# The first norm's conditioning chunks split between TensorE and VectorE, a T5 bias table built on GpSimd's queue, and a later forget bias

## The chip, the cores and the metric

One core of a Trainium2 chip runs the whole program. The metric is the device time of one execution in microseconds (us); the times below are medians of three runs. TensorE (PE) does matmuls, VectorE (DVE) elementwise work and reductions, ScalarE (ACT) activations and copies, GpSimd (POOL) small elementwise work, and SyncE (SP) issues the DMAs.

## What is computed

Two layers of a transformer block on 256 tokens of width 1024, in float32. Each layer has a mixer (three kinds of attention side by side) and a SwiGLU. A conditioning vector `c` gives, by a matmul with `w_ada`, a shift, a scale and a gate for both halves of each layer:

```python
mod = (silu(c) @ w_ada[l] + b_ada[l])
shift_a, scale_a, gate_a, shift_f, scale_f, gate_f = split(mod, 6)
h = rmsnorm(x, g_mix_pre[l]) * (1.0 + scale_a) + shift_a
x = x + gate_a * rmsnorm(mixer(h), g_mix_post[l])
h = rmsnorm(x, g_ffn_pre[l]) * (1.0 + scale_f) + shift_f
x = x + gate_f * rmsnorm(swiglu(h), g_ffn_post[l])
```

In the mixer, "fox" attention (4 heads) adds a cumulated forget logit to its scores, "moba" attention (4 heads; at 256 tokens there is one block) adds a T5 bias that depends on the distance of query and key only, and "mla" attention (8 heads) goes through low-rank latents and rope.

## The kernel before

Weights stream from HBM in pieces of 128x1024 (512 KB). `split` (lines 101 to 103) turns each into a high part `wh` on ScalarE (L102) and a low part `wl` on VectorE (L103), and a product is three matmuls (L148 to L150 or L170 to L172). The program is written as a dataflow; a planner puts each engine's instructions into one fixed order before the run, by its own estimate of when each is ready, with the order of writing as priority. An engine works through its list in that order and waits at each instruction for what it needs. SP is the only DMA issuer.

The conditioning comes in chunks. Twelve chunks per half layer: eight of 256 columns (128 of shift, 128 of scale, for one of eight groups of model columns) and four of the gate. One chunk is two loads `adaw` of 512 KB (`ada_load`, L250). There are two ways to compute one (`ada_chunk`, L260): on VectorE as two multiply-and-reduce instructions against `crow`, the conditioning vector spread over all partitions (L266), or on TensorE as eight matmuls on four column groups (L274, `adap`, two records each), a copy on ScalarE (L277, `adasb`), two transposes (L286, `adac`) and a small reduce on VectorE (L287). `on_dve` (L37) picks the way; the first norm's eight chunks of layer 0 all go by TensorE. `ada_scale` then adds the bias (L294) and forms the factor (L296) in `ab`.

Layer 0's first norm and first projection are interleaved (`phase_a`, L578, here "phase A"): for each of eight groups `kc` of model columns, the chunk is conditioned, x is transposed and normalised by a matmul with a diagonal (L949, `xT`), `modulate` (L364) makes `hv` on ScalarE and the parts `h0aH` and `h0aL` on VectorE (L367 to L369), and seven column slots are projected with three matmuls each. TensorE's order in this stage is written out by hand (`chain`): the conditioning and the transpose of group kc+1 stand before slot 0 of group kc, `adac` of kc+1 before slot 2. The diagonal needs the row factor `rs`, a power on GpSimd (L343), one for each 128 tokens.

After phase A come the latents, the values (`value1`), and the T5 bias (`t5_bias`, L226): one matmul of a one-hot table gives the band of biases by distance, four DMAs write it to DRAM 32 times per head (`scr`, L242), and one DMA (L245) reads it back with a step of 383 elements per partition, so that row p comes out shifted by p: `mobab`. The forget logits are cumulated, and `rows_of` (L299) writes them to DRAM (L306) and reads them back spread over all partitions (`gk`, L309), also on SP. `fox_bias` (L725) makes the bias of one fox head in two pieces: L729 for the first 128 queries, which is ordered after the last maximum seen so far (`last["max"]`, set at L435), and L732 for the others, which has no such order.

Then eight pairs of heads: four mla, two fox, two moba. A pair's scores (L458, L460) need `qx` (L763, VectorE) for mla; softmax is L433 to L445 on VectorE, ScalarE and GpSimd. Between the pairs stand pieces of projection (`qkp`) and the remaining conditioning chunks (`fill`).

Of the kernel before, what the change touches and what calls it, by code (L numbers as in the profile page):

```python
# [36 lines left out]
def on_dve(l, which, j):  # L37

    if which == 1 and j < KC:
        return j in MIX_DVE[l]  # L40
    return j >= KC or l > 0


@with_exitstack
def block_kernel(ctx, tc, A, out):
# [16 lines left out]
    def pm(name, n=512):  # L62
        return psum.tile([P, n], F32, tag="pm", bufs=2, name=name)
# [120 lines left out]
    x = const.tile([P, 2, D], F32, name="x")  # L184
    for t in range(2):
        SP.dma_start(x[:, t, :], A["x"][:, t, :])
    shp = const.tile([P, 896], F32, name="shp")
    tri, ones, ktab = (shp[:, i * P:(i + 1) * P] for i in range(3))
    mask, qtab = (shp[:, 384 + i * S:384 + (i + 1) * S] for i in range(2))
    bfor = const.tile([P, L, 4], F32, name="bfor")  # L190
# [32 lines left out]

    mobab = const.tile([P, 4, S], F32, name="mobab")

    def t5_bias():  # L226
        tab = wk.tile([P, 4], F32, tag="tab", bufs=1, name="tab")
        SP.dma_start(tab, A["t5"])
        oneh = wk.tile([P, 384], F32, tag="e", bufs=4, name="oneh")
        SP.dma_start(oneh, A["k_onehot"])  # L230
        trep = wk.tile([P, 4, 32], F32, tag="kt", bufs=2, name="trep")
        DVE.tensor_copy(trep, tab[:, :, None].to_broadcast([P, 4, 32]))
        tp = pg("tp")
        for hd in range(4):
            PE.matmul(tp[32 * hd:32 * hd + 32, :384], trep[:, hd, :], oneh, start=True, stop=True,
                      tile_position=(0, 32 * hd))
        band = wk.tile([P, 384], F32, tag="e", bufs=4, name="band")
        ACT.activation(band, tp[:, :384], AF.Copy)

        scr = dram.tile([4, 4, 32, 384], F32, name="scr")  # L240
        for q in range(4):
            SP.dma_start(scr[:, q, :, :], band)  # L242
        base = scr[:, :, :, :]
        toep = bass.AP(base.tensor, base.offset + 127, [[383, P], [P * 384, 4], [1, S]])
        SP.dma_start(mobab, toep)  # L245


    loaded = {}
# [11 lines left out]
    def ada_chunk(l, which, j):  # L260
        raws = loaded.pop((l, which, j), None) or ada_load(l, which, j)
        if on_dve(l, which, j):

            sb = wk.tile([P, 2], F32, tag="adasum", bufs=4, name="adasum")
            for u in range(2):
                i = DVE.tensor_tensor_reduce(out=raws[u], in0=raws[u], in1=crow, op0=ALU.mult, op1=ALU.add,  # L266
                                             scale=1.0, scalar=0.0, accum_out=sb[:, u:u + 1])
                if last.get("ffn"):
                    order_after(i, last["wl"])
            return sb  # L270
        ps = pm("adap", 256)
        for kc in range(KC):
            g = kc % 4
            chain(PE.matmul(ps[32 * g:32 * g + 32, :], crep[:, kc, :], raws[kc // 4][:, g * 256:(g + 1) * 256],  # L274
                            start=kc < 4, stop=kc >= 4, tile_position=(0, 32 * g)))
        sb = wk.tile([P, 256], F32, tag="adasb", bufs=1, name="adasb")
        ACT.activation(sb, ps, AF.Copy)  # L277
        return sb

    def ada_columns(l, which, j, sb, dst):  # L280

        if on_dve(l, which, j):
            return sb
        ps = pm("adac", 256)
        for u in range(2):
            chain(PE.transpose(ps[:, u * P:(u + 1) * P], sb[:, u * P:(u + 1) * P], ident))  # L286
        DVE.tensor_reduce(dst, ps.rearrange("p (u g r) -> p u g r", u=2, g=4)[:, :, :, 0], op=ALU.add,  # L287
                          axis=mybir.AxisListType.X)
        return dst
# [37 lines left out]
    def gate_step(l, which, j):  # L327
        ada_gate(l, which, j)

    def scale_step(l, which, kc, sb=None):  # L330
        if kc == 0:
            ABs[l, which] = act.tile([P, KC, 2], F32, tag="ab", bufs=3, name=f"ab{l}{which}")
        ada_scale(l, which, ABs[l, which], kc, ada_chunk(l, which, kc) if sb is None else sb)


# [186 lines left out]
    def mixer(l, h, prepare, fill, after):  # L522
# [55 lines left out]
        def phase_a():  # L578
# [11 lines left out]
            for kc in range(AHEAD):  # L590
                load(kc)
            state["chain"] = True
            adas[0] = ada_chunk(0, 0, 0)
            turn(0)
            scaled(0)
# [95 lines left out]
        if l == 0:  # L691
            for i, ps in enumerate(rest):
                qk_out(ps, i)
            w1.extend(value_weights(l))
            for t in range(2):
                value1(t)
            t5_bias()


        kx = act.tile([P, 8, S], F32, tag="kx", name="kx")  # L700
# [24 lines left out]
        def fox_bias(hd):  # L725
            fb = wk.tile([P, 384], F32, tag="fb", bufs=2, name="fb")
            gk = gks[:, hd]

            i = DVE.scalar_tensor_tensor(fb[:, 0:P], gk[:, 0:P], gqs[:, 2 * hd:2 * hd + 1], mask[:, P:S],  # L729
                                         op0=ALU.subtract, op1=ALU.add)  # L730
            order_after(i, last["max"])
            DVE.scalar_tensor_tensor(fb[:, P:384], gk, gqs[:, 2 * hd + 1:2 * hd + 2], mask,  # L732
                                     op0=ALU.subtract, op1=ALU.add)
            return fb

        if l == 0:
# [259 lines left out]
def _constants():  # L996
    import numpy as np
    f = np.float32
    p = np.arange(P)
    j = np.arange(S)  # L1000
    out = {}
    out["k_tri"] = (p[:, None] <= p[None, :]).astype(f)
    out["k_ones"] = np.ones((P, P), f)
    out["k_mask"] = np.where(j[None, :] <= P + p[:, None], 0.0, NEG).astype(f)
# [11 lines left out]
    oneh = np.zeros((P, 384), f)  # L1016
    oneh[np.where(dist >= 0, _bucket(dist), 32), np.arange(384)] = 1.0
    out["k_onehot"] = oneh
    shapes = np.concatenate([out.pop(k) for k in ("k_tri", "k_ones", "k_ktab", "k_mask", "k_qtab")], axis=1)
    out["shapes"] = shapes  # L1020
    return out


def _layout(inputs):
# [4 lines left out]
    o["t5"] = np.concatenate([g["t5_table"], np.full((1, 4), NEG, np.float32), np.zeros((P - 33, 4), np.float32)])  # L1029
    o["b_forget"] = g["b_forget"]  # L1030

    def kchunks(w):
# [5 lines left out]
    for l in range(L):  # L1038
        for which in range(2):
            parts = [g["w_ada"][l][:, (3 * which + i) * D:(3 * which + i + 1) * D] for i in range(3)]  # L1040
            for j in range(12):
# [5 lines left out]
                if on_dve(l, which, j):  # L1047
# [69 lines left out]
```

## Time and profile before

| | us |
|---|---|
| median of three runs | 676.29 |
| lowest and highest of them | 673.01 and 677.72 |
| the profiled execution | 677.55 |
| its span, first to last instruction | 675.7 |

The rows further down come from that one profiled execution. Times count from the span's start. A row of the timeline has start, duration, engine, line, operation, what it writes and reads, and in brackets how long the engine stood idle before it and what ended that. The chain of waits is followed back from the last instruction, each step to what released it.

### The profile page before, as it was taken

The page shows a single profiled execution, that of the slowest core. Times are in us where ns is not written, and L with a number is a line of the kernel's source. Part 1 is how long each engine was busy: PE and PEld are TensorE (multiplying, and loading weights), DVE is VectorE, ACT ScalarE, POOL GpSimd, SP SyncE. Part 2 cuts the span into 40 slices and gives each one's busy share as a digit, 9 for nine tenths or more (in the row PEclk, how much of TensorE's full clock was granted, in tenths as well). Part 3 has the DMA queues.
Part 4 walks back from the last instruction along what each step waited for, and adds up shares of the span by engine and source line. Part 5 has one row for each costly group of instructions (what it writes and reads, how often), then busy time and mean ns, then how long its engine had stood idle before and what let it go on. Part 6 is the DMA issues. An engine that isn't in the chain of part 4 may idle for free.

```text
span 675.7 us, 12112 instructions
## 1 busy us (share of the span) xinstructions
PE 638.3 (94%) x4543; PEld 564.7 (84%) x4543; DVE 451.2 (67%) x969; ACT 365.7 (54%) x758; POOL 52.8 (8%) x90
## 2 busy tenths in 40 slices
PE   7988769999999999999998999899899999999996
PEld 5877658567999999999978988768799999999994
DVE  2557277878867777797658864875878755555543
ACT  4348436868644444443467764886764444444431
POOL 1000011431000000000001011250100000000000
PEclk8999979999999999999999999999999999999999
DMA  8968586786478898898845865651568676565511
GB/s 311 407 214 287 161 315 221 266 289 214 123 255 308 288 357 307 312 325 287 303 157 173 270 229 185 219 189 64 187 196 271 223 237 182 183 185 183 185 60 63
DMA packets 44410, 155.29 MB, mean 230 GB/s; under 512 B 5136, under 2 KB 6464, under 8 KB 44352
## 3 DMA queue, kind: packets, MB, share of 16 engines
q1 hardware_dynamic: 44352, 154.52, 67.7%
q8 instruction: 36, 0.59, 0.4%
q14 instruction: 22, 0.18, 0.1%
HBM read 152.64 MB, written 1.86 MB: 229 GB/s over the span
## 4 chain that ended last, share of the span: by engine, by line
PE 76%; DVE 8%; DMA 6%; ACT 3%; POOL 3%; issue 2%; SPq 0%; DVEq 0%; POOLq 0%; ACTq 0%
PE gu L148 11%; PE gu L149 11%; PE gu L150 11%; PE y L172 8%; PE y L170 8%; PE y L171 8%; DMA adaw<-in_w_ada_dram 4%; DVE wl L103 3%; PE adap L274 2%; PE o L478 2%; DMA scr<-band 2%; POOL rs L343 1%; PE qkp L150 1%; PE s L460 1%; PE qkp L148 1%
## 5 line engine op out<-in xcount | busy, mean ns | idle before, releaser
L103 DVE TENSOR_TENSOR wl<-raw_gu,wh 128x1024 fp32r<-128x1024 f32 (+1 forms) x100 | 108.5, 1095 | 67.8 <-ACT wh L102 66.8
L102 ACT ACTIVATE wh<-raw_gu 128x1024 fp32r<-128x1024 f32 (+1 forms) x100 | 94.2, 956 | 92.0 <-PE gu L149 62.5
L148 PE MATMUL gu<-h0fL,wh 128*128 128x256 f32 x304 | 86.2, 283 | 0.0
L148 PE MATMUL gu<-h1fL,wh 128*128 128x256 f32 x304 | 86.2, 283 | 0.0
L149 PE MATMUL gu<-h0fH,wh 128*128 128x256 f32 x304 | 86.0, 283 | 0.0
L149 PE MATMUL gu<-h1fH,wh 128*128 128x256 f32 x304 | 86.0, 283 | 0.0
L150 PE MATMUL gu<-h0fH,wl 128*128 128x256 f32 x304 | 86.0, 283 | 0.0
L150 PE MATMUL gu<-h1fH,wl 128*128 128x256 f32 x304 | 86.0, 283 | 0.0
L266 DVE CUSTOM_DVE_ANT_0 adaw<-adaw,crow 128x1024 f32<-128x1024 f32 x64 | 77.9, 1227 | 11.8 <-DMA adaw<-in_w_ada_dram 11.7
L102 ACT ACTIVATE wh<-raw_dn 128x1024 fp32r<-128x1024 f32 x44 | 46.6, 1060 | 54.8 <-issue 33.3
L171 PE MATMUL y<-wh,hid 128*128 128x512 f32 x176 | 69.6, 396 | 0.0
L170 PE MATMUL y<-wh,hid 128*128 128x512 f32 x176 | 69.5, 396 | 0.0
L172 PE MATMUL y<-wl,hid 128*128 128x512 f32 x176 | 69.5, 395 | 0.0
L103 DVE TENSOR_TENSOR wl<-raw_dn,wh 128x1024 fp32r<-128x1024 f32 x44 | 53.6, 1223 | 21.8 <-ACT wh L102 21.7
L149 PEld LDWEIGHTS gu<-h1fH,wh 128*128 128x128 f32 x304 | 58.3, 192 | 0.4
L149 PEld LDWEIGHTS gu<-h0fH,wh 128*128 128x128 f32 x304 | 58.3, 192 | 0.4
L148 PEld LDWEIGHTS gu<-h1fL,wh 128*128 128x128 f32 x304 | 58.2, 192 | 0.4
L148 PEld LDWEIGHTS gu<-h0fL,wh 128*128 128x128 f32 x304 | 58.2, 192 | 0.4
L150 PEld LDWEIGHTS gu<-h1fH,wl 128*128 128x128 f32 x304 | 58.3, 192 | 0.0
L150 PEld LDWEIGHTS gu<-h0fH,wl 128*128 128x128 f32 x304 | 58.3, 192 | 0.0
L343 POOL TENSOR_TENSOR rs<-rs,mhalf 128x1 f32<-128x1 f32 x16 | 11.0, 688 | 439.4 <-DVE rs L342 439.4
L172 PEld LDWEIGHTS y<-wl,hid 128*128 128x128 f32 x176 | 33.0, 188 | 8.0
(331 smaller groups left out, 1482.2 us busy)
## 6 DMA issues: line engine op xcount, KB each, us to landing
adaw<-in_w_ada_dram SPq DMA_DIRECT2D x96, 512.0 KB
raw_gu<-in_w_gu_dram SPq DMA_DIRECT2D x88, 512.0 KB
raw_dn<-in_w_dn_dram SPq DMA_DIRECT2D x44, 512.0 KB
raw_out<-in_w_out_dram SPq DMA_DIRECT2D x16, 512.0 KB
raw_b<-in_w_b_dram SPq DMA_DIRECT2D x12, 512.0 KB
raw_a<-in_w_a_dram SPq DMA_DIRECT2D x8, 448.0 KB
raw_uq<-in_w_uq_dram SPq DMA_DIRECT2D x4, 512.0 KB
raw_vm<-in_w_vm_dram SPq DMA_DIRECT2D x4, 512.0 KB
```

The lines of the kernel that those rows point to most:

```text
L102: ACT.activation(dst_h, src, AF.Copy)
L103: return DVE.tensor_tensor(dst_l, src, dst_h.bitcast(F32), op=ALU.subtract)
L148: chain(PE.matmul(ps, w[0], x[1], start=start, stop=False))
L149: chain(PE.matmul(ps, w[0], x[0], start=False, stop=False))
L150: chain(PE.matmul(ps, w[1], x[0], start=False, stop=stop))
L170: PE.matmul(ps, x[1], w[0], start=start, stop=False)
L171: PE.matmul(ps, x[0], w[0], start=False, stop=False)
L172: PE.matmul(ps, x[0], w[1], start=False, stop=stop)
L266: i = DVE.tensor_tensor_reduce(out=raws[u], in0=raws[u], in1=crow, op0=ALU.mult, op1=ALU.add, scale=1.0, scalar=0.0, accum_out=sb[:, u:u + 1])
L274: chain(PE.matmul(ps[32 * g:32 * g + 32, :], crep[:, kc, :], raws[kc // 4][:, g * 256:(g + 1) * 256], start=kc < 4, stop=kc >= 4, tile_pos ...
L343: POOL.tensor_tensor(r, r, mhalf, op=ALU.pow)
L478: PE.matmul(o[64 * u:64 * u + 64, lo:lo + P], v[:, u * 64:(u + 1) * 64], ps[u][:, i * P:(i + 1) * P], start=start, stop=stop, tile_positio ...
```

## The change

Three parts. First, for layer 0's first norm the chunk is laid out so that its first load holds the shift's columns and its second the scale's: the shift goes by TensorE with 128 columns (8 matmuls, one transpose), the scale by one multiply-and-reduce on VectorE that writes straight into `ab`. Second, the T5 band is made at the start of the program: all its transfers are issued by GpSimd, `scr` holds the band once (4 rows of 384), two loads of 256 KB read it back with a step of one element per partition, that is, with the rows in reverse order, and later, at the old place of `t5_bias`, two matmuls with a reversed identity (`flip`, loaded with the other constants) turn it and two copies fill `mobab`. Third, both pieces of the forget bias are ordered after `last["max"]`.

```diff
+def halves(l, which, j):
+    return l == 0 and which == 0 and j < KC
...
-    def t5_bias():
-        tab = wk.tile([P, 4], F32, tag="tab", bufs=1, name="tab")
-        SP.dma_start(tab, A["t5"])
-        oneh = wk.tile([P, 384], F32, tag="e", bufs=4, name="oneh")
-        SP.dma_start(oneh, A["k_onehot"])
-        trep = wk.tile([P, 4, 32], F32, tag="kt", bufs=2, name="trep")
-        DVE.tensor_copy(trep, tab[:, :, None].to_broadcast([P, 4, 32]))
+    def t5_load():
+        tab = wk.tile([64, 4], F32, tag="tab", bufs=1, name="tab")
+        POOL.dma_start(tab, A["t5"])
+        oneh = wk.tile([64, 384], F32, tag="e", bufs=4, name="oneh")
+        POOL.dma_start(oneh, A["k_onehot"])
         tp = pg("tp")
-        for hd in range(4):
-            PE.matmul(tp[32 * hd:32 * hd + 32, :384], trep[:, hd, :], oneh, start=True, stop=True,
-                      tile_position=(0, 32 * hd))
...
-        scr = dram.tile([4, 4, 32, 384], F32, name="scr")
-        for q in range(4):
-            SP.dma_start(scr[:, q, :, :], band)
-        base = scr[:, :, :, :]
-        toep = bass.AP(base.tensor, base.offset + 127, [[383, P], [P * 384, 4], [1, S]])
-        SP.dma_start(mobab, toep)
+        PE.matmul(tp[0:4, :384], tab, oneh, start=True, stop=True)
+        band = wk.tile([4, 384], F32, tag="e", bufs=4, name="band")
+        ACT.activation(band, tp[0:4, :384], AF.Copy)
+        scr = dram.tile([4, 384], F32, name="scr")
+        POOL.dma_start(scr, band)
+        base = scr[:, :]
+        turned = [wk.tile([P, 512], F32, tag="yg", bufs=2, name="t5rows") for _ in range(2)]
+        for n in range(2):
+            POOL.dma_start(turned[n], bass.AP(base.tensor, base.offset + n * 768, [[1, P], [384, 2], [1, S]]))
+        return turned
+
+    def t5_bias(turned):
+        for n in range(2):
+            ps = pg("t5b")
+            PE.matmul(ps, flip, turned[n], start=True, stop=True)
+            ACT.activation(mobab[:, 2 * n:2 * n + 2, :], ps.rearrange("p (h j) -> p h j", h=2), AF.Copy)
+
+    t5 = t5_load()
...
+        if halves(l, which, j):
+            ps = pm("adap", P)
+            for kc in range(KC):
+                g = kc % 4
+                chain(PE.matmul(ps[32 * g:32 * g + 32, :], crep[:, kc, :], raws[0][:, kc * P:(kc + 1) * P],
+                                start=kc < 4, stop=kc >= 4, tile_position=(0, 32 * g)))
+            sb = wk.tile([P, 256], F32, tag="adasb", bufs=1, name="adasb")[:, :P]
+            ACT.activation(sb, ps, AF.Copy)
+            DVE.tensor_tensor_reduce(out=raws[1], in0=raws[1], in1=crow, op0=ALU.mult, op1=ALU.add,
+                                     scale=1.0, scalar=0.0, accum_out=ABs[l, which][:, j, 1:2])
+            return sb
...
+        if halves(l, which, j):
+            ps = pm("adac", P)
+            chain(PE.transpose(ps, sb, ident))
+            DVE.tensor_reduce(dst[:, 0:1], ps.rearrange("p (g r) -> p g r", g=4)[:, :, 0], op=ALU.add,
+                              axis=mybir.AxisListType.X)
+            return dst
...
-            t5_bias()
+            t5_bias(t5)
...
-            i = DVE.scalar_tensor_tensor(fb[:, 0:P], gk[:, 0:P], gqs[:, 2 * hd:2 * hd + 1], mask[:, P:S],
-                                         op0=ALU.subtract, op1=ALU.add)
-            order_after(i, last["max"])
-            DVE.scalar_tensor_tensor(fb[:, P:384], gk, gqs[:, 2 * hd + 1:2 * hd + 2], mask,
-                                     op0=ALU.subtract, op1=ALU.add)
+            for t, sl, m in ((0, slice(0, P), mask[:, P:S]), (1, slice(P, 384), mask)):
+                i = DVE.scalar_tensor_tensor(fb[:, sl], gk[:, :sl.stop - sl.start],
+                                             gqs[:, 2 * hd + t:2 * hd + t + 1], m, op0=ALU.subtract, op1=ALU.add)
+                order_after(i, last["max"])
```

## Rows read from the trace of the kernel before

**Rows 1.** The page: span, part 1 (busy by engine), part 4 (chain by engine).

```profile
span 675.7 us, 12112 instructions
...
PE 638.3 (94%) x4543; PEld 564.7 (84%) x4543; DVE 451.2 (67%) x969; ACT 365.7 (54%) x758; POOL 52.8 (8%) x90
...
PE 76%; DVE 8%; DMA 6%; ACT 3%; POOL 3%; issue 2%; SPq 0%; DVEq 0%; POOLq 0%; ACTq 0%
```

**Rows 2.** Stretches: length; PE, PEld, DVE, ACT, POOL busy us; clock; DMA share; GB/s.

```profile
15.00:40.00 25.00, 25.00 (x248) 20.68 (x249) 11.37 (x34) 10.16 (x17) 0.00 (x0) 0.99 1.02 402
...
65.00:80.00 15.00, 13.79 (x107) 12.29 (x105) 6.91 (x22) 9.93 (x23) 1.67 (x4) 1.00 0.50 172
80.00:85.00 5.00, 0.66 (x4) 0.21 (x3) 0.00 (x0) 0.57 (x2) 0.00 (x0) 0.87 0.80 232
85.00:95.00 10.00, 7.14 (x35) 5.98 (x36) 7.43 (x23) 0.80 (x2) 0.00 (x0) 0.55 1.01 355
```

**Rows 3.** Chain of waits, 60 to 97 us: start, us, what.

```profile
66.90 0.49 ACT band L238
...
69.29 10.34 DMA scr<-band
...
80.12 5.44 DMA gk<-rowsgk
```

**Rows 4.** Timeline of VectorE, 77 to 88 us.

```profile
77.17 0.17 DVE L443 RECIPROCAL ri<-sm 128x2 f32<-128x2 f32 x1 [0.71 <-ACT e L441]
85.59 0.48 DVE L732 SCALAR_TENSOR_TENSOR fb<-gk,gqs,shp 128x256 f32<-128x256 f32 x1 [8.25 <-DMA gk<-rowsgk]
...
87.12 0.68 DVE L763 TENSOR_TENSOR qx<-qp,qt 128x512 f32<-128x512 f32 x1
87.77 1.23 DVE L266 CUSTOM_DVE_ANT_0 adaw<-adaw,crow 128x1024 f32<-128x1024 f32 x1
```

**Rows 5.** Timeline of TensorE, 65 to 92 us.

```profile
65.87 0.85 PE L235 MATMUL tp<-oneh,trep 128*32 128x384 f32 x8
...
87.86 1.22 PE L458 MATMUL s<-kx,qx 128*128 128x128 f32 x4 [7.19 <-DVE qx L763]
```

**Rows 6.** Chain of waits in phase A, one group of columns.

```profile
19.56 1.00 PE adap L274 x16
20.56 0.64 PE xT L949 x4
...
21.92 0.22 PE adac L286 x2
...
23.93 1.00 PE adap L274 x16
```

**Rows 7.** Timeline of VectorE in phase A, one group of columns.

```profile
17.82 0.17 DVE L287 TENSOR_REDUCE ab<-adac 128x2 f32<-128x8 f32 x1 [2.36 <-PE adac L286]
...
18.10 1.09 DVE L103 TENSOR_TENSOR wl<-raw_a,wh 128x896 fp32r<-128x896 f32 x1
19.11 0.15 DVE L296 SCALAR_TENSOR_TENSOR ab<-ab,first 128x1 f32<-128x1 f32 x1
...
20.28 0.43 DVE L369 TENSOR_TENSOR h0aL<-hv,h0aH 128x256 fp32r<-128x256 f32 x1
22.17 0.17 DVE L287 TENSOR_REDUCE ab<-adac 128x2 f32<-128x8 f32 x1 [1.47 <-PE adac L286]
```

**Rows 8.** The page, part 6: DMA issues with their size.

```profile
adaw<-in_w_ada_dram SPq DMA_DIRECT2D x96, 512.0 KB
...
raw_a<-in_w_a_dram SPq DMA_DIRECT2D x8, 448.0 KB
```

**Rows 9.** Timeline of GpSimd, 4 to 14 us.

```profile
7.86 0.56 POOL L343 TENSOR_TENSOR rs<-rs,mhalf 128x1 f32<-128x1 f32 x1 [6.56 <-DVE rs L342]
10.79 0.55 POOL L343 TENSOR_TENSOR rs<-rs,mhalf 128x1 f32<-128x1 f32 x1 [2.37 <-DVE rs L342]
```

**Rows 10.** Chain of waits, the start: the first conditioning load.

```profile
2.58 8.56 DMA adaw<-in_w_ada_dram
```

**Rows 11.** Timeline of ScalarE, 65 to 82 us.

```profile
77.52 1.06 ACT L102 ACTIVATE wh<-raw_b 128x1024 fp32r<-128x1024 f32 x1 [0.39 <-ACT e L441]
```

More of the change, by code (lines that the diff above doesn't have):

```diff
@@ L186, in block_kernel @@
         SP.dma_start(x[:, t, :], A["x"][:, t, :])
-    shp = const.tile([P, 896], F32, name="shp")
+    shp = const.tile([P, 1024], F32, name="shp")
+    flip = shp[:, 896:1024]
     tri, ones, ktab = (shp[:, i * P:(i + 1) * P] for i in range(3))
@@ L224, in block_kernel @@
     mobab = const.tile([P, 4, S], F32, name="mobab")
-    def t5_bias():
-        tab = wk.tile([P, 4], F32, tag="tab", bufs=1, name="tab")
-        SP.dma_start(tab, A["t5"])
-        oneh = wk.tile([P, 384], F32, tag="e", bufs=4, name="oneh")
-        SP.dma_start(oneh, A["k_onehot"])
-        trep = wk.tile([P, 4, 32], F32, tag="kt", bufs=2, name="trep")
-        DVE.tensor_copy(trep, tab[:, :, None].to_broadcast([P, 4, 32]))
-        tp = pg("tp")
-        for hd in range(4):
-            PE.matmul(tp[32 * hd:32 * hd + 32, :384], trep[:, hd, :], oneh, start=True, stop=True,
-                      tile_position=(0, 32 * hd))
-        band = wk.tile([P, 384], F32, tag="e", bufs=4, name="band")
-        ACT.activation(band, tp[:, :384], AF.Copy)
-        scr = dram.tile([4, 4, 32, 384], F32, name="scr")
-        for q in range(4):
-            SP.dma_start(scr[:, q, :, :], band)
-        base = scr[:, :, :, :]
-        toep = bass.AP(base.tensor, base.offset + 127, [[383, P], [P * 384, 4], [1, S]])
-        SP.dma_start(mobab, toep)
+    def t5_load():
[3 more added lines that the diff above has]
+        POOL.dma_start(oneh, A["k_onehot"])
+        tp = pg("tp")
+        PE.matmul(tp[0:4, :384], tab, oneh, start=True, stop=True)
[14 more added lines that the diff above has]
+    t5 = t5_load()
     loaded = {}
@@ L328, in gate_step, with new_ab @@
         ada_gate(l, which, j)
+    def new_ab(l, which):
+        ABs[l, which] = act.tile([P, KC, 2], F32, tag="ab", bufs=3, name=f"ab{l}{which}")
     def scale_step(l, which, kc, sb=None):
-        if kc == 0:
-            ABs[l, which] = act.tile([P, KC, 2], F32, tag="ab", bufs=3, name=f"ab{l}{which}")
+        if (l, which) not in ABs:
+            new_ab(l, which)
         ada_scale(l, which, ABs[l, which], kc, ada_chunk(l, which, kc) if sb is None else sb)
@@ L592, in phase_a @@
             state["chain"] = True
+            new_ab(0, 0)
             adas[0] = ada_chunk(0, 0, 0)
@@ L1003, in _constants @@
     out["k_ones"] = np.ones((P, P), f)
+    out["k_flip"] = np.eye(P, dtype=f)[::-1].copy()
     out["k_mask"] = np.where(j[None, :] <= P + p[:, None], 0.0, NEG).astype(f)
@@ L1015, in _constants @@
     dist = 255 - np.arange(384)
-    oneh = np.zeros((P, 384), f)
+    oneh = np.zeros((64, 384), f)
     oneh[np.where(dist >= 0, _bucket(dist), 32), np.arange(384)] = 1.0
     out["k_onehot"] = oneh
-    shapes = np.concatenate([out.pop(k) for k in ("k_tri", "k_ones", "k_ktab", "k_mask", "k_qtab")], axis=1)
+    shapes = np.concatenate([out.pop(k) for k in ("k_tri", "k_ones", "k_ktab", "k_mask", "k_qtab", "k_flip")], axis=1)
     out["shapes"] = shapes
@@ L1028, in _layout @@
     o["x"] = g["x"][0].reshape(2, P, D).transpose(1, 0, 2)
-    o["t5"] = np.concatenate([g["t5_table"], np.full((1, 4), NEG, np.float32), np.zeros((P - 33, 4), np.float32)])
+    o["t5"] = np.concatenate([g["t5_table"], np.full((1, 4), NEG, np.float32), np.zeros((64 - 33, 4), np.float32)])
     o["b_forget"] = g["b_forget"]
@@ L1046, in _layout @@
                     ch = parts[2][:, (j - KC) * 256:(j - KC + 1) * 256]
-                if on_dve(l, which, j):
+                if halves(l, which, j):
+                    ch = np.concatenate([ch[:, :P].reshape(KC, P, P).transpose(1, 0, 2).reshape(P, D),
+                                         ch[:, P:].T], axis=1)
+                elif on_dve(l, which, j):
                     ch = ch.T.reshape(2, P, D).transpose(1, 0, 2)
```

## The prediction, made before the change was run

> **What bounds the kernel now.** I read the page first. TensorE is busy for 94% of the span and holds 76% of the chain that ended last; VectorE has 8% and DMA 6% [rows 1]. So a saving off TensorE's path is worth nothing in most places, and I look for the stretches in which TensorE is slow for a reason that the change touches. The table of stretches [rows 2] gives two. From 15 to 40 us (the first norm and the first projection, phase A) TensorE is full and the DMA engines are full as well (share 1.02, 402 GB/s). From 80 to 85 us TensorE works 0.66 of 5 us, and from 85 to 95 us its granted clock is 0.55, close to the 1.2 GHz level, where 15 to 40 and 65 to 80 us show 0.99 and 1.00, the 2.4 GHz level. The chain of waits explains the second: scr<-band takes 10.34 us, SP stands behind it, and the load gk<-rowsgk (5.44 us) can only start at 80.12 [rows 3]. VectorE's own order does the rest: after ri at 77.17 it sits at the bias piece fb (L732) until gk lands at 85.56, 8.25 us idle, with the wl split and qx queued behind fb [rows 4]. TensorE then waits 7.19 us for qx [rows 5].
>
> **Phase A, part by part.** One chunk takes 23.93 - 19.56 = 4.37 us, and it is all TensorE's: adap 1.00, xT 0.64, adac 0.22, and 2.5 us of projection [rows 6]. The change halves adap's columns (256 to 128, still 16 records) and takes one of two transposes from adac. Half of each is 0.50 + 0.11 = 0.61; some of adap is weight loads, which don't shrink, so I take 0.56, and TensorE's chunk becomes 3.81 us. Seven intervals give 3.9 us.
>
> VectorE gets one reduce over 128x1024 per chunk. The same operation is in the trace (L266): 1.22 us [rows 4]. In the loop VectorE has L287 at 17.82, wl 1.09, L296, and h0aL ending at 20.71, then nothing until the next L287 at 22.17 [rows 7]. The gap is 1.47 us, so the reduce just fits there, if the planner puts it there. When the period shrinks to 3.8 the gap shrinks to 0.9 and VectorE is about as late as TensorE. What is then late next is the path adac, L287, wl, L296, hv, h0aL, next projection. From the start of L287 to the end of h0aL it is 2.89 us now [rows 7]; TensorE covers it with the other five slots (15 matmuls), adap and xT, which lose the 0.50. If the reduce lands inside that path instead, it adds 1.22 there and the period is about 5.0 us, 0.65 above now.
>
> DMA: a chunk is two adaw loads and one raw_a, 512 + 512 + 448 KB [rows 8] = 1.51 MB, at 402 GB/s 3.75 us. That is no slower than the new TensorE chunk, but with no room. T5's loads come on top, now early: 96 KB of one-hot rows and 512 KB of turned rows, 0.62 MB or 1.5 us of a stream that is already full. The early gain: the scale half no longer has to pass TensorE, and adap 0 needs only the first load, perhaps 0.8 us at chunk 0. Sum: -3.9 - 0.8, and +1.2 for most of T5's bytes, **-3.5 us**; bounds -4.7 (T5 hidden, all kept) and +4.6 (reduce on the path, 7 x 0.65).
>
> On those bytes a rule is worth weighing, since it speaks against the move to another queue. The row shows the share of the 16 DMA engines at 1.02 and nothing issued by GpSimd, so a second queue is not seen [rows 2]. The Trainium skill (DMA: Bandwidth & Descriptors, "Issuing engines are not separate DMA queues") says that transfers issued by sync, scalar or GpSimd run on the same 16 engines and interleave, and that another issuer saves only issue time. By it the 1.5 us stay in the stream; had GpSimd's queue room of its own, phase A would come to -4.7 and the total to 664.1.
>
> **GpSimd's queue at the start.** t5_load issues five DMAs on it: tab, oneh, then scr after band, then two turned loads after scr has landed. Behind these waits, in the order in which they are written, stand the two powers (L343) that now run at 7.86 and 10.79 [rows 9]; for them wait diag, xT 0 and so chunk 0. If the planner puts the powers first, nothing is lost. If not, they start after scr's landing. The trace has no DMA issued by GpSimd, so from both sides: 0, or the loads as slow as the first adaw (8.56) and scr as slow as the old one (10.34) [rows 3, 10], a hold of some 12 us. scr is now 6 KB and not four times 192 KB, so I stay near the low end: **+0.2**.
>
> **The stall.** SP no longer waits for scr, and both fb pieces follow last["max"], so VectorE meets no gk at 77. Next late there: wh from 77.52 to 78.58 on ScalarE [rows 11], wl 1.22, qx 0.68, so qx ends at 80.5 and the scores start there and not at 87.86: 7.4 us. Then the clock: 7.14 us of TensorE work between 85 and 95 ran at 0.55 [rows 2]; at full clock it is 3.9, which is 3.2 more. Together 10.6. Not all goes through: the ada reduces that VectorE has there (L266 at 87.77) need loads that SP issued during the stall, and ScalarE and GpSimd work from 95 us on is serial. I take **-9.0**; bounds -10.6 and -3 (VectorE meets such a load instead, about as late as gk was).
>
> **T5 turned on TensorE.** Removed: trep, tp (0.85), band's place on ScalarE (0.49), six transfers on SP. Added before the pairs: two f32 matmuls of 512 columns and two copies to mobab. By xT (0.64 for two of 128 columns) they are 4 x 0.64 = 2.6 us, by tp (384 columns) 2 x 0.85 x 512/384 = 2.3; net 1.4 to 1.7 on TensorE, which has 1.2 us free between 65 and 80 [rows 2, 5, 6]. ScalarE: 2 x 0.49 x 512/384 - 0.49 = 0.8, beside 5 us idle there [rows 2, 3]. I take **+0.8**; bounds 0 and 1.7.
>
> **Forget bias later.** A piece fb of 0.48 [rows 4] that ran early now stands between the last maximum of the MLA pairs and the first fox pair, once or twice per layer. VectorE is busy there, TensorE has projections and y to do: **+0.5** for both layers, bounds 0 and 1.9.
>
> **Sum.** -3.5 + 0.2 - 9.0 + 0.8 + 0.5 = -11.0. The profiled execution took 677.55 us (span 675.7 [rows 1], 1.85 around it), 1.26 above the median of 676.29 and inside the spread of the three runs. On the profiled one this gives 666.55, on the median 665.3, which I forecast.
>
> **Rivals.**
> *The reduce lies on phase A's path.* For it: VectorE is left with under 1 us free per chunk, and now already runs wl ahead of L296, so the planner does put a long piece into that path [rows 7]. Against: the reduce needs only its load, which is ahead by more than a chunk in the loop, so it can go early. Price: phase A at about +2 (half the chunks) in place of -3.5, total 670.8.
> *Another wait takes the stall's place.* For it: VectorE's order is fixed beforehand, and the reduces at 87.77 and after depend on loads by SP [rows 4]. Against: SP, free of scr, issues them earlier than now, and the DMA share between 65 and 80 is only 0.50 [rows 2]. Price: stall part at -3, total 671.3.
> *Slower: GpSimd's queue held at scr.* The powers stand behind scr's landing; loads that land like the first adaw at 2.58 + 8.56 = 11.1, tp and band 1.3 more, scr 10.34: 22.8, then the two powers of 0.55 end at 23.9, where the second ends now at 11.34 [rows 3, 9, 10]. That delays chunk 0 by 12.6 us, and TensorE, idle that long, would come back at half clock as after 80 us, 3.2 more. Total 665.3 + 15.8 = 681.1. It decides from a hold and clock loss of 11 us together. Against: scr's size.
>
> **Chances.** Forecast 0.68 (its own range 660 to 669.5), reduce on the path 0.13, another wait 0.12, slower 0.07. One per cent, about what a measurement of this kernel can tell from no change, is 6.8 us: faster means below 669.5, slower above 683. The slower rival at its price is 0.7% above now, and over 683 only if the hold is some 2 us longer: about half of its chance. So faster has the forecast and a little from the lower sides of the two middle rivals, 0.70; slower 0.04; same the rest, 0.26. The range's upper end, 674, holds both middle rivals with room. Its lower end: the good bounds of all terms (-4.7, 0, -10.6, 0, 0) give 661, and the lowest of the three runs lay 3.3 below their median, so 657.
>
> **What would show it.** Right: chunks of phase A spaced 3.8 us by adap; the reduce before L287, not between L287 and h0aL; the powers near 8 and 11 us; VectorE without an idle time over 2 us between 74 and 82; granted clock 1.00 in that stretch; gk landing with nobody waiting. Wrong: adap spaced 4.4 or more, a power after 13 us, or a new VectorE wait on an adaw load of over 4 us in the pairs.

## The result, and the profile after

The change takes 666.1 us (median of four executions, 664.74 to 669.92) against 676.29 us: ratio 0.9867, interval 0.9837 to 0.9896. That is 10.2 us less, where 11.0 were forecast, and over one per cent at both ends of the interval. The profiled execution took 665.89 us with a span of 664.0, so span against span the gain is 11.7 us. Of all executions in this document one was in a slow state (t5_fb, 676.11 us, 1.65% above that kernel's fastest); it is left out of that kernel's median and ratio. The sum came out; whose gain it is came out otherwise than written, and most of what follows is about that.

The page of the change, against [rows 1]: TensorE's busy time falls by 3.7 us while the span falls by 11.7, so most of the gain is idle time that went away.

```profile
span 664.0 us, 12102 instructions
...
PE 634.6 (96%) x4533; PEld 562.9 (85%) x4533; DVE 461.9 (70%) x984; ACT 366.9 (55%) x760; POOL 60.1 (9%) x95
...
PE 77%; DVE 8%; DMA 5%; ACT 4%; POOL 3%; issue 2%; SPq 0%; DVEq 0%; POOLq 0%; ACTq 0%
```

The stretches of [rows 2], in the change:

```profile
15.00:40.00 25.00, 25.00 (x270) 22.20 (x268) 21.17 (x52) 11.12 (x19) 1.54 (x2) 0.95 1.03 403
65.00:80.00 15.00, 13.14 (x92) 11.48 (x91) 9.32 (x26) 8.21 (x21) 2.59 (x4) 1.00 0.94 299
80.00:85.00 5.00, 5.00 (x46) 4.67 (x45) 4.56 (x18) 3.03 (x8) 1.14 (x1) 1.00 0.96 364
85.00:95.00 10.00, 7.98 (x52) 6.14 (x51) 5.87 (x22) 5.63 (x20) 4.97 (x8) 0.83 0.73 253
```

From 80 to 85 us TensorE is full, where it had 0.66 of 5 us, at a granted clock of 1.00; from 85 to 95 the clock is 0.83 and no longer 0.55. The DMA engines carry between 65 and 80 us what they carried after 85: share 0.94 where it was 0.50, 0.73 where it was 1.01.

Two rows of the chain of waits in phase A, one interval apart, answer to [rows 6]: 3.83 us for 4.37, and 0.57 for adap's 1.00.

```profile
20.40 0.57 PE adap L287 x16
...
24.23 0.57 PE adap L287 x16
```

VectorE in that interval, against [rows 7] (L310 is the small reduce, L401 makes h0aL, L291 is the new one, the multiply-and-reduce, called "the reduce" below):

```profile
20.45 0.42 DVE L401 TENSOR_TENSOR h0aL<-hv,h0aH 128x256 fp32r<-128x256 f32 x1
20.79 1.22 DVE L291 CUSTOM_DVE_ANT_0 adaw<-adaw,crow 128x1024 f32<-128x1024 f32 x1
...
22.48 0.16 DVE L310 TENSOR_REDUCE ab<-adac 128x1 f32<-128x4 f32 x1 [0.46 <-PE adac L309]
```

The reduce stands behind h0aL and ahead of the small reduce, and VectorE waits 0.46 us before the latter: the reduce is off the path, as hoped.

GpSimd at the start, against [rows 9]. The DMA `scr` stands ahead of the second power, which runs at 12.64 and not at 10.79:

```profile
7.81 0.56 POOL L375 TENSOR_TENSOR rs<-rs,mhalf 128x1 f32<-128x1 f32 x1 [4.93 <-DVE rs L374]
12.04 0.58 POOL L243 DMA_DIRECT2D scr<-band  x1 [3.67 <-ACT adasb L290]
12.64 0.72 POOL L375 TENSOR_TENSOR rs<-rs,mhalf 128x1 f32<-128x1 f32 x1
17.56 1.54 POOL L247 DMA_DIRECT2D t5rows<-scr  x2 [4.19 <-DMA scr<-band]
```

SP's queue, against [rows 3]: gk goes out at 70.17, not at 80.12, and two conditioning loads 0.9 us behind it.

```profile
70.17 0.33 SPq L338 DMA_DIRECT2D gk<-rowsgk  x1
...
71.03 0.89 SPq L268 DMA_DIRECT2D adaw<-in_w_ada_dram  x2
```

VectorE, against [rows 4]: no wait for gk. What is left are waits for conditioning loads, the longest of 2.38 us.

```profile
73.61 1.23 DVE L277 CUSTOM_DVE_ANT_0 adaw<-adaw,crow 128x1024 f32<-128x1024 f32 x1 [1.00 <-DMA adaw<-in_w_ada_dram]
...
76.40 0.68 DVE L795 TENSOR_TENSOR qx<-qp,qt 128x512 f32<-128x512 f32 x1
79.45 1.23 DVE L277 CUSTOM_DVE_ANT_0 adaw<-adaw,crow 128x1024 f32<-128x1024 f32 x1 [2.38 <-DMA adaw<-in_w_ada_dram]
```

TensorE, against [rows 5]: the matmuls that turn T5 ran at 43.28, ahead of phase A's last group of columns, and pair 1's scores start at 78.65, not at 87.86.

```profile
43.28 1.88 PE L253 MATMUL t5b<-t5rows,shp 128*128 128x512 f32 x4
...
78.65 0.71 PE L490 MATMUL s<-kx,qx 128*128 128x128 f32 x4
```

### The profile page after: what moved, and what is told of

It reads as the page before. It is cut to its first block, busy times and chain, and to the rows that moved or that the text cites. A ratio compares the mean times of both kernels' runs of the same rounds, so it can differ in the third digit from the quotient of the medians.

```text
span 664.0 us, 12102 instructions
## 1 busy us (share of the span) xinstructions
PE 634.6 (96%) x4533; PEld 562.9 (85%) x4533; DVE 461.9 (70%) x984; ACT 366.9 (55%) x760; POOL 60.1 (9%) x95
## 4 chain that ended last, share of the span: by engine, by line
PE 77%; DVE 8%; DMA 5%; ACT 4%; POOL 3%; issue 2%; SPq 0%; DVEq 0%; POOLq 0%; ACTq 0%
PE gu L153 11%; PE gu L154 11%; PE gu L155 11%; PE y L175 7%; PE y L176 7%; PE y L177 7%; DMA adaw<-in_w_ada_dram 3%; DVE wl L108 2%; PE o L510 2%; ACT wh L107 1%; PE qkp L153 1%; PE qkp L154 1%; PE qkp L155 1%; POOL rs L375 1%; DMA x<-in_x_dram 1%
## 5 line engine op out<-in xcount | busy, mean ns | idle before, releaser
L277 DVE CUSTOM_DVE_ANT_0 adaw<-adaw,crow 128x1024 f32<-128x1024 f32 x64 | 77.9, 1229 | 10.7 <-DMA adaw<-in_w_ada_dram 10.5
L154 PEld LDWEIGHTS gu<-h1fH,wh 128*128 128x128 f32 x304 | 58.2, 192 | 0.4
L154 PEld LDWEIGHTS gu<-h0fH,wh 128*128 128x128 f32 x304 | 58.2, 192 | 0.4
L153 PEld LDWEIGHTS gu<-h1fL,wh 128*128 128x128 f32 x304 | 58.2, 191 | 0.4
L153 PEld LDWEIGHTS gu<-h0fL,wh 128*128 128x128 f32 x304 | 58.2, 191 | 0.4
L155 PEld LDWEIGHTS gu<-h1fH,wl 128*128 128x128 f32 x304 | 58.2, 192 | 0.0
L155 PEld LDWEIGHTS gu<-h0fH,wl 128*128 128x128 f32 x304 | 58.2, 192 | 0.0
```

Of the source, the lines that this page charges most:

```text
L153: chain(PE.matmul(ps, w[0], x[1], start=start, stop=False))
L154: chain(PE.matmul(ps, w[0], x[0], start=False, stop=False))
L155: chain(PE.matmul(ps, w[1], x[0], start=False, stop=stop))
```

## The experiments

Twelve kernels were run. The table has their medians, their ratios to the kernel before on the same chip, and some starts from TensorE's timeline in the profiled execution of each: the end of phase A (first matmul with `zero` behind the loop), the scores of pairs 0, 1 and 3, and the first FFN rows of layer 0 (L170 of the kernel before). FFN is the SwiGLU half of a layer.

| kernel | median us | ratio (95%) | phase A ends | pair 0 | pair 1 | pair 3 | FFN |
|---|---|---|---|---|---|---|---|
| before | 676.3 | 1 | 50.1 | 73.1 | 87.9 | 114.6 | 168.9 |
| the change | 666.1 | 0.9867 (0.9837 to 0.9896) | 47.5 | 69.7 | 78.7 | 100.4 | 156.2 |
| fb_only | 676.1 | 0.9995 (0.9969 to 1.0022) | 49.4 | 72.4 | 79.9 | 109.9 | 164.2 |
| halves_only | 679.6 | 1.0039 (1.0012 to 1.0066) | 45.9 | 72.6 | 87.7 | 112.3 | 171.9 |
| t5_only | 667.1 | 0.9840 (0.9804 to 0.9875) | 49.8 | 71.8 | 79.8 | 101.8 | 160.2 |
| halves_fb | 679.0 | 1.0045 (1.0020 to 1.0070) | 45.3 | 71.3 | 78.7 | 109.9 | 165.7 |
| halves_t5 | 669.4 | 0.9898 (0.9846 to 0.9949) | 48.4 | 70.9 | 80.5 | 101.8 | 160.3 |
| t5_fb | 668.7 | 0.9899 (0.9864 to 0.9934) | 49.8 | 71.6 | 80.0 | 100.0 | 158.3 |
| t5_queue | 677.5 | 1.0021 (0.9997 to 1.0046) | 48.7 | 74.0 | 90.2 | 110.6 | 168.9 |
| t5_small_late | 674.4 | 0.9983 (0.9955 to 1.0011) | 49.2 | 73.9 | 87.4 | 109.3 | 164.9 |
| t5_big_early | 671.1 | 0.9922 (0.9891 to 0.9952) | 53.8 | 77.6 | 85.7 | 107.1 | 166.6 |
| powers_first | 669.4 | 0.9881 (0.9851 to 0.9912) | 47.0 | 70.0 | 78.6 | 100.2 | 158.6 |
| table_in_loop | 669.5 | 0.9906 (0.9870 to 0.9941) | 47.5 | 70.2 | 78.2 | 100.5 | 159.0 |
| scale_on_dve | 668.7 | 0.9887 (0.9853 to 0.9921) | 48.9 | 71.2 | 80.1 | 103.5 | 159.8 |

Two cautions. The ratio is not the quotient of the two medians and can differ from it by 0.3% (t5_only: 667.1 to 676.0 would be 0.987); the twelve were run on three chips, so across the table ratios are compared and not times. And a start comes from one execution: the kernel before, fb_only and t5_queue differ only behind phase A, and it ends at 50.1, 49.4 and 48.7, so a difference of a microsecond between two starts says little.

### One part of the change alone

**fb_only**: the later forget bias, the other two parts as before. The order is the only difference:

```diff
+            for t, sl, m in ((0, slice(0, P), mask[:, P:S]), (1, slice(P, 384), mask)):
...
+                order_after(i, last["max"])
```

> Only the later forget bias, the rest as before. Theory (VectorE's order makes the stall): VectorE no longer meets gk at 77 us, the second pair's scores start near 80.5 and not at 87.86; SP is still held at scr until about 79.6, so the gate loads after it come late and take some of it back: 6 to 8 us less than before, 668 to 670. Rival (SP's hold alone makes the stall, through the loads): the second pair's scores come at 86 or later, and the time falls by under 2 us.

Measured: 0.9995, no gain. VectorE indeed no longer meets gk, and pair 1 starts 8 us earlier. But SP is still held at scr, so the conditioning loads go out only at 80.45, and VectorE waits for one of them. SP's and then VectorE's timeline in fb_only:

```profile
79.46 0.39 SPq L250 DMA_DIRECT2D mobab<-scr  x1
79.94 0.46 SPq L332 DMA_DIRECT2D gk<-rowsgk  x1
80.45 1.60 SPq L262 DMA_DIRECT2D adaw<-in_w_ada_dram  x3
```

```profile
87.79 1.22 DVE L271 CUSTOM_DVE_ANT_0 adaw<-adaw,crow 128x1024 f32<-128x1024 f32 x1 [8.11 <-DMA adaw<-in_w_ada_dram]
```

A wait of 8.11 us takes the place of one of 8.25 [rows 4]. The bias was only the first instruction to meet the held queue. This is the prediction's rival "another wait takes the stall's place", true for this part alone. In the profiled execution the FFN is 4.7 us earlier and the end 2.2; in the medians nothing is left. So the starts came as the theory had them and the time as the rival had it.

**halves_only**: the divided chunks, the other two parts as before (in t5_only and t5_fb the same function returns False):

```diff
 def halves(l, which, j):
     return l == 0 and which == 0 and j < KC
```

> Only the divided conditioning chunks. Theory: adap is spaced 3.83 us as in the full change; with nothing of T5 on GpSimd's queue the second power runs near 10.8 us and not at 12.64, so phase A's last zero matmul comes 4 to 4.5 us before that of the kernel before (50.06), and the stall at 80 us stays: 3 to 4.5 us less than before, 672 to 673. Rival (phase A is bound by its loads and the split adds nothing): the end of phase A moves by under 2 us, time within 2 us of before.

Measured: 1.0039, slower, which neither the theory nor the rival had. Phase A does end 4.2 us earlier, as expected; at pair 0 0.6 us of it is left. Rows of VectorE's timeline and of the chain of waits between the two show a part of why:

```profile
51.71 0.75 DVE L108 TENSOR_TENSOR wl<-raw_v,wh 128x584 fp32r<-128x584 f32 x1
```

```profile
52.53 5.11 DMA raw_vm<-in_w_vm_dram
```

The loads of weights share four buffers, and SP waits 4.2 us for one of them until VectorE's split of raw_v ends at 52.46. Only then do the value weights go out (at 50.16 in the kernel before), and ScalarE splits them from 57.66 on: before it was 57.67.

The forget bias then waits for gk as before:

```profile
83.60 0.49 DVE L759 SCALAR_TENSOR_TENSOR fb<-gk,gqs,shp 128x256 f32<-128x256 f32 x1 [7.73 <-DMA gk<-rowsgk]
```

A faster phase A runs into splits and loads that are not earlier. Between pair 3 and the FFN another 5.3 us are lost against before (59.6 us for 54.3); the section on what was not expected has a part of that.

**t5_only**: T5 early, small and on GpSimd's queue, the other two parts as before.

```diff
-            t5_bias()
+    t5 = t5_load()
...
+            t5_bias(t5)
```

> Only the T5 table on GpSimd's queue, turned on TensorE; fb keeps its old order. Theory: SP is free of scr, gk is issued near 73 us instead of 80.12 and lands near 79, so VectorE's wait at fb shrinks from 8.25 to about 2 us; the power behind scr costs about 2 us at the start: 3 to 5 us less than before, 671 to 673. Rival (the stall is fb's order alone): fb still waits 6 us or more, and the time is that of before or up to 2 us above it.

Measured: 0.9840, a larger gain than expected (667.1 us, where the theory gave 671 to 673). It is the lowest ratio of all, but its interval overlaps that of the change, and by the medians the change gains more (10.2 us, here 8.9). With the old order of the forget bias VectorE now waits for gk for less than a microsecond:

```profile
77.35 0.49 DVE L765 SCALAR_TENSOR_TENSOR fb<-gk,gqs,shp 128x256 f32<-128x256 f32 x1 [0.94 <-DMA gk<-rowsgk]
```

### Two parts

> The change with T5 as before. Theory (with SP held at scr neither of the other two parts brings anything; VectorE waits for adaw in place of gk): VectorE idles at least 5 us for adaw or gk between 75 and 97 us, and the time is 674 to 680 us. Rival (the two parts help each other): 669 to 672 us.

> The change without the later forget bias. Theory (with SP free, phase A's gain of 2.5 us arrives at pair 0 and a third of it is lost again further on): 665 to 667 us, the forget bias waits under 1.5 us for gk. Rival (divided chunks bring nothing at the end, as alone): 668 to 672 us. Rival (the forget bias's order is needed): the bias waits over 3 us and the time is over 669 us.

> The change with the conditioning chunks of phase A as before. Theory (T5's move is practically the whole gain): the end of phase A stays at about 50 us, pair 1 begins at 79 to 80.5 us, and the time is 666 to 668 us, that of T5's move alone. Rival (chunks and T5 each bring their part): 669 to 671 us.

Each leaves one part of the change out. Measured: halves_fb 1.0045, as the theory had it, with VectorE again waiting for a conditioning load:

```profile
86.17 1.23 DVE L271 CUSTOM_DVE_ANT_0 adaw<-adaw,crow 128x1024 f32<-128x1024 f32 x1 [7.62 <-DMA adaw<-in_w_ada_dram]
```

halves_t5 came to 669.4, some 2 us above the time that the theory gave and within the first rival's; t5_fb came to 668.7, between the theory's 668 and the rival's 669, and decides nothing. Now all eight combinations are there. The four with T5 moved have a mean ratio of 0.9876, the four without 1.0020: T5's move is worth 1.4%, or 9.7 us. Worked out the same way, the divided chunks are worth +0.29% (0.9962 with, 0.9934 without) and the later bias +0.07%. Neither of these two is a gain that the runs show. The four pairs behind the chunks' figure are +0.39%, +0.50% and +0.58%, and -0.32% where both other parts are present (the change against t5_fb). That one gain is not yet there at pair 3, which starts at 100.4 in the change and at 100.0 in t5_fb; the 2.1 us at the FFN come behind it, where the last pair's scales on GpSimd differ (see the last section). Among the four with T5 all intervals overlap; which of them is the fastest stays open.

### What of T5's move it is

T5's move is three things: another queue, fewer bytes (scr once and not 32 times per head), an earlier place. The queue and the form were tried at the old place, and the early place with the old form on the new queue.

**t5_queue**: the kernel before, with scr and mobab issued by GpSimd at their old place.

```diff
-            SP.dma_start(scr[:, q, :, :], band)
+            POOL.dma_start(scr[:, q, :, :], band)
...
-        SP.dma_start(mobab, toep)
+        POOL.dma_start(mobab, toep)
```

> The kernel before with one thing changed: the four scr DMAs and the mobab DMA are issued on GpSimd's queue, with all their bytes, at their old place. Theory (SP's hold at these DMAs is what costs, not their bytes nor the table's late place): gk is issued at about 70 us instead of 80, the scores of pair 1 begin at 79 to 82 us instead of 87.9, pair 0's softmax scales on GpSimd start at about 80 instead of 76.6, and the time is 667 to 670 us. Rival (the smaller table or its earlier place is what gains): the gk and adaw transfers share the DMA engines with the 10 us bounce as before, pair 1 stays behind 85 us and the time is 673 to 677 us.

Measured: 1.0021, and my theory (SP's hold is what costs) fell. gk goes out at 72.60, 7.5 us earlier, and pair 1 is not earlier for it: the bounce and all that SP now issues run together. The stretch of t5_queue in which that is so:

```profile
75.00:80.00 5.00, 5.00 (x29) 4.82 (x28) 0.94 (x6) 0.00 (x0) 0.44 (x1) 0.66 1.00 393
```

The DMA engines are full (share 1.00, 393 GB/s), and VectorE, whose order now has a conditioning reduce ahead of pair 0's softmax, waits 4.12 us for it; pair 0's scale on GpSimd comes 6.5 us later than before and takes 2.44 us, and pair 1 starts at 90.2.

```profile
80.46 1.23 DVE L266 CUSTOM_DVE_ANT_0 adaw<-adaw,crow 128x1024 f32<-128x1024 f32 x1 [4.12 <-DMA adaw<-in_w_ada_dram]
```

```profile
83.10 2.44 POOL L444 TENSOR_SCALAR e<-e,ri 128x128 f32<-128x128 f32 x1 [2.74 <-DVE ri L443]
```

The same scale in the kernel before, on GpSimd's timeline:

```profile
76.56 0.38 POOL L444 TENSOR_SCALAR e<-e,ri 128x128 f32<-128x128 f32 x1 [65.21 <-DVE ri L443]
```

By pair 3 this kernel is all the same 4.0 us ahead of the kernel before (110.6 for 114.6), and loses them again up to the FFN, where the last pair's scales on GpSimd take longer (6.0 us for 4.0, see the last section). So the end shows no gain, and the stretch behind the hold shows one.

**t5_small_late**: T5's new small form, at its old place and on SP's queue.

```diff
-    t5 = t5_load()
...
-            t5_bias(t5)
+            t5_bias(t5_load())
```

(In `t5_load` each `POOL.dma_start` is `SP.dma_start`.)

> T5's new small form (one row per head through DRAM, turned on TensorE) alone, but at its old place and on SP's queue; chunks and forget bias as before. Theory (what costs is that the old bounce keeps both SP's queue and the DMA engines for 10 us just ahead of the first pairs; its bytes and its length matter, not its place): the hold at scr shrinks to 2 to 5 us, gk is issued at 71 to 75 us, and the time is 667 to 671 us. Rival (only the early place helps, any wait for scr on SP costs the same): 673 to 677 us.

Measured: 0.9983, with the hold gone as the theory had it and the time as the rival had it. gk goes out at 69.64 and VectorE has no wait over 0.2 us for any load until 105 us. Yet pair 1 starts at 87.4. GpSimd's timeline, then TensorE's:

```profile
79.44 2.56 POOL L476 TENSOR_SCALAR e<-e,ri 128x256 f32<-128x256 f32 x1
```

```profile
79.94 0.60 PE L482 MATMUL pt<-first,e 128*128 128x128 f32 x4
82.05 0.44 PE L482 MATMUL pt<-first,e 128*128 128x128 f32 x2 [1.52 <-POOL e L476]
...
87.41 0.61 PE L489 MATMUL s<-kx,qx 128*128 128x128 f32 x4
```

TensorE waits for a slow scale, and then it does what its list has next: twelve matmuls of pair 0's `o` and 17 of `qkp`, at a granted clock of 0.73 (82 to 86 us), before the scores, although `qx` is there since 83.7. In the change two `qkp` and two `o` stand between the transposes and the scores. So between two pairs the fixed list of an engine can cost as much as a late load. Here the small bounce was over before gk went out (its last load was issued at 62.5 and landed within 6.5 us), SP was free, and still nothing was won: an early end of the bounce is not enough by itself.

**t5_big_early**: the old form with all its bytes, at the start, on GpSimd's queue.

```diff
+    t5_bias()
...
-            t5_bias()
```

(In `t5_bias` each `SP.dma_start` is `POOL.dma_start`.)

> The kernel before with its whole old T5 bias (replicated table, four scr writes, one mobab read) issued at the start on GpSimd's queue; nothing else changed. Theory (bytes and hold ahead of the first pairs cost, the start has room for them): GpSimd's queue is held for scr and mobab before about 30 us, the first adap comes up to 4 us later, the pairs begin as in T5's move alone but for that, 668 to 672 us. Rival (the form's bytes cost wherever they are, or the second power waits behind them): 674 to 682 us.

Measured: 0.9922, as the theory had it. GpSimd, in t5_big_early:

```profile
12.53 2.87 POOL L242 DMA_DIRECT2D scr<-band  x4 [2.64 <-ACT band L238]
15.42 0.57 POOL L345 TENSOR_TENSOR rs<-rs,mhalf 128x1 f32<-128x1 f32 x1
```

The second power is 4.6 us later and phase A ends 3.8 us later, and still 5.7 us are won; pair 1 comes 8.1 us behind pair 0 and not 14.7. (Its profiled execution took 676.2 us, the longest of its ten; the starts in the table are of that one.) About half of the move's gain (0.8 of 1.6%) thus comes with the early place, old form and all; the other queue at the old place, or the new form at the old place, brings nothing at the end that can be told from zero. These last two kernels also got another list: in the kernel before, the change and t5_big_early TensorE has pair 1's scores four matmuls behind pair 0's transposes, in t5_queue and t5_small_late it has many more in between. So their zero is not the queue's or the form's alone, and how the planner comes to either list is not shown. The new form at the early place on SP's queue was not tried.

### Could the start be better?

**powers_first**, **table_in_loop** and **scale_on_dve** build on the whole change. The first writes the table behind the norm of x and orders scr behind the second power:

```diff
+        order_after(POOL.dma_start(scr, band), last["pow"])
```

> The full change with the GpSimd DMA to scr ordered behind the second power. Theory (the hold at scr delays chunk 0): the second power runs near 11 us and not at 12.64, the first projection starts 1.5 to 2 us earlier, and this goes through to the end: 664 to 665 where the full change has 666.1. Rival (phase A waits for its loads anyway): the first projection moves, but adap of the last group does not, under 0.5 us in all.

Measured: 0.9881, no gain over the change's 0.9867. The power is back at 11.23, phase A ends 0.5 us earlier than in the change, and pair 3 starts 0.3 us earlier; at the FFN it is 2.4 us later. Of the 1.41 us that the power gains (12.64 to 11.23) at most 0.5 gets through: in the chain of waits chunk 0 now hangs on its first weights:

```profile
3.05 9.46 DMA raw_a<-in_w_a_dram
```

**table_in_loop** adds that one of T5's two loads (`tab`) is ordered behind the cast of `zero`, and that table, scr and rows are made after the third group:

```diff
+        order_after(POOL.dma_start(tab, A["t5"]), zero_cast)
...
+                if kc == 2:
+                    t5.extend(t5_load(*t5_in))
```

> The whole change, with T5's two loads on GpSimd behind the cast of zero, and the table, scr and the rows made in phase A after its third group, behind both powers. By the traces: the second power is back at about 10.8 us (12.64 in the change), the first adap at about 14.5, the end of phase A 1 to 1.9 us earlier than the change's 47.5. If that arrives at the end: 664 to 665.5 us, ratio to before 0.981 to 0.985. Rival (as with the scr behind the power: the gain is lost in the second half of the mixer to GpSimd's scales beside VectorE's ada reductions): 666.5 to 670 us.

Measured: 0.9906, no gain, the rival's time. The power is at 10.84, and phase A ends at 47.5 as in the change: the table's matmul now takes 0.73 us within the loop, and the load of raw_a sets chunk 0 here too. The other load (`oneh`), which the edit does not order, was issued ahead of the cast of `zero` (1.35 and 2.12), so the cast came no earlier than in the change.

**scale_on_dve** adds that the softmax scales of layer 0's last pair run on VectorE:

```diff
-        POOL.tensor_scalar(e[:, 0:P], e[:, 0:P], ri[:, 0:1], 1.0, op0=ALU.mult, op1=ALU.mult)
+        eng.tensor_scalar(e[:, 0:P], e[:, 0:P], ri[:, 0:1], 1.0, op0=ALU.mult, op1=ALU.mult)
```

> The former kernel with the softmax scales of layer 0's last pair on VectorE instead of GpSimd. Theory (four scales took 4.9 to 6.0 us on GpSimd beside VectorE's ada reductions, against some 1.7 alone, and the last transposes of the mixer wait for them): these transposes come 2 to 3 us earlier and the FFN's first matmuls 0.5 to 2.5 us earlier than in the former kernel: 663 to 666 us. Rival (TensorE has the output projection to do meanwhile, or VectorE pays it back): the former's time within 1 us.

Measured: 0.9887, not to be told from the former. The mechanism is there: the last transposes of the mixer start 26.1 us after pair 3 (129.54), 29.7 in table_in_loop (130.17), and from pair 3 to the FFN it takes 56.3 us for 58.4. But in the profiled execution pair 0 came 1 us later and pair 3 came 3 us later, and the medians differ by 0.9 us. None of the twelve kernels can be told to beat the change.

## Why the prediction was right, and where it was not

**Phase A, -3.5.** The period was right (3.83 for 3.81), and so was the place of the reduce. The end of phase A came 2.6 us earlier, and pair 0 3.4. As a term of the sum it was wrong: over four pairs of kernels that differ in this part alone it is +0.29% in the mean, not -0.5%. Two steps failed. The 0.8 us at chunk 0 did not come: the adap of [rows 6] starts at 20.40 in the change and at 19.56 before. And the gain at phase A's end was carried through to the program's end without naming what is late next behind the loop. In halves_only it is the load of raw_vm, which waits for a buffer until a split frees one.

**T5's bytes in phase A, +1.2 in that term.** Not seen. The period is 3.83 with 0.62 MB more at 403 GB/s, and in t5_big_early, with 0.79 MB written and 0.5 MB read, adap still starts every 4.37 to 4.38 us from 23.64 us on. A DMA share of 1.0 was not a sign that one more transfer lengthens the stage: TensorE set the period, and the loads ran ahead of it. The rule weighed in the prediction (the Trainium skill, DMA: Bandwidth & Descriptors, "Issuing engines are not separate DMA queues") agrees with the trace in its own matter: with GpSimd issuing as well the rate stays at 403 GB/s, 402 before. But bytes in a full stream were no time here.

**GpSimd's queue, +0.2.** The planner did put the DMA ahead of the second power, which the prediction left open; the power came 1.85 us later. powers_first, with the power back, ends phase A 0.5 us earlier, which is the term's measure as far as one start can give it. The slower rival, a hold of 12 us, did not occur because GpSimd's wait for scr's landing (4.19 us) stands behind the power.

**The stall, -9.0.** The size was right: from pair 0 to pair 3 the change takes 30.7 us, the kernel before 41.4, so 10.7 less, at the far end of the bounds (-10.6); 1.5 us are given back up to the FFN (55.8 us from pair 3, 54.3 before), which leaves 9.2. The cause was half right. The sentence "SP no longer waits for scr, and both fb pieces follow last["max"], so VectorE meets no gk at 77" gave two reasons where one would do: with T5 moved alone the bias waits 0.94 us; with the bias moved alone VectorE waits 8.11 us for the next load. And even SP's hold is not the whole of it, since freeing SP without moving the bounce brought nothing at the end (t5_queue), nor did a bounce that was small and over before gk went out (t5_small_late). All that paid had T5 at the start. That the early place pays is shown; why it does is not isolated, since both kernels with the bounce altered at its old place also got another list on TensorE.

**T5 turned on TensorE, +0.8.** The size was right, the place was not. The planner put these matmuls ahead of phase A's last group of columns (1.88 us at 43.28). In the kernel before TensorE has a gap there that would take them in, but the divided chunks shrink it. TensorE's timeline before and in halves_only:

```profile
47.48 0.36 PE L148 MATMUL cq<-h0aL,wh 128*128 128x256 f32 x1 [1.69 <-ACT wh L102]
```

```profile
43.27 0.36 PE L153 MATMUL cq<-h0aL,wh 128*128 128x256 f32 x1 [0.62 <-DVE h0aL L395]
```

From the last adap to the first matmul with `zero` it is 7.1 us in halves_only (38.75 to 45.86) and 8.0 in halves_t5 (40.44 to 48.41): the turn costs 0.9 there. With undivided chunks it costs nothing (8.7 both in the kernel before and in t5_only). I had looked for room only at the place where they are written.

**Forget bias later, +0.5.** Its mean effect of +0.07% is 0.5 us, too small for these runs to show.

**The rivals.** "Reduce on the path" did not occur. "Another wait" occurred in part: three waits of 0.42 to 2.38 us for conditioning loads from 69 to 80 us, under the 4 us that the prediction named as the sign of failure. Two of its signs of being right did not come: the wait of 2.38 us at 79.45, where none over 2 us was to be, and the second power at 12.64 and not near 11. So the total was right by one term, T5's, that was larger than my sum had it (some 9.7 us by the combinations; t5_only has 8.9 by its medians and 10.8 by its ratio) and two, of -3.5 and +0.5, that brought nothing. T5's own terms in the sum (stall, turn and GpSimd's queue) came to -8.0, so that the errors cancel to within 0.8 us of the total is luck.

## What to carry to other kernels

When a queue is held, ask which instructions would meet the hold one after the other: the one that the trace shows waiting is only the first, and to move it exposes the next. Freeing a queue is not freeing the DMA engines: here the bounce through DRAM paid when it moved to the start, ahead of a stage whose period TensorE sets, and that stage took its bytes even at full DMA share. It paid neither on another queue nor in a smaller form at its old place, where the engines' lists and slow scales took the gain back. A saving in one stage is a term of the sum only if the next stage's loads and splits are ready for it.

## What was not expected of the hardware

A softmax scale on GpSimd takes 0.37 us (128x128) or 0.47 (128x256) when VectorE does not run long instructions with two inputs in SBUF, and up to 2.56 us when it does (conditioning reduces, and the split `wl`). The change's timeline of VectorE and then of GpSimd, at the last pair:

```profile
123.93 1.22 DVE L277 CUSTOM_DVE_ANT_0 adaw<-adaw,crow 128x1024 f32<-128x1024 f32 x1
125.08 1.22 DVE L277 CUSTOM_DVE_ANT_0 adaw<-adaw,crow 128x1024 f32<-128x1024 f32 x1
```

```profile
123.99 2.46 POOL L476 TENSOR_SCALAR e<-e,ri 128x128 f32<-128x128 f32 x1 [2.21 <-DVE ri L475]
126.43 0.48 POOL L477 TENSOR_SCALAR e<-e,ri 128x256 f32<-128x256 f32 x1
```

The scale starts 0.06 us after the first reduce and ends 0.15 us after the second: it lasts as long as the two together. The Trainium skill (SBUF — State Buffer, "Who interferes with whom") says that a VectorE instruction with two inputs in SBUF contends with a GpSimd instruction that reads SBUF, and the one that issues second is held; the trace agrees, with 2.46 us for 0.37, as far as the first reduce goes. The second started 1.1 us after the scale, and the scale outlasted it as well. The four scales of this pair take 4.9 us in the change, 6.0 in powers_first, table_in_loop and halves_only, and 4.0 before; the same four on VectorE itself (scale_on_dve) take 0.28 and 0.35 each. Between pair 3 and the FFN the change needs 55.8 us and those three 58.4 to 59.6. All kernels with these scales on GpSimd fall into three groups: scales of 4.0 us and 54.3 from pair 3 to the FFN (the kernel before, fb_only), 4.9 us and 55.6 to 55.8 (the change, halves_fb, t5_small_late), 6.0 us and 58.2 to 59.6 (the eight others). So a part of what sets the change apart from t5_only, halves_t5 and t5_fb appears in this stretch, far behind the parts that were combined. That the scales are all of this difference is not shown: it is larger than the scales' own.
